# Where a weight block is split into two halves: the loads and ScalarE in place of VectorE

## The chip, the cores and the metric

One core of one Trainium2 chip runs the program. The metric is the device time of one execution in microseconds. The engines are TensorE (PE; PEld is its weight load), VectorE (DVE), ScalarE (ACT), GpSimd (POOL) and SyncE (SP), which here only issues DMAs.

## What is computed

Two layers of a hybrid backbone over 256 context tokens and 512 latent tokens of 1024 features, in float32. A norm modulated by a conditioning vector feeds one wide projection; its columns go to four token mixers (attention, Fourier mixing, a state-space scan S5, retention); each mixer's result is projected back, weighted by a gate, summed and projected once more; then comes an MLP of width 4096. Layer 1 computes the context tokens only as far as the latent ones read them.

```
for l in range(DEPTH):
    ...
    zl = split_cols(hl @ w_in[l], full_sizes)
    k_l, v_l = mla_keys(zl[0], zl[1], mla_kv_norm[l], mla_w_ukv[l], mla_qk_norm_k[l], rows, cols)
    q_l = mla_queries(zl[5], mla_q_norm[l], mla_w_uq[l], mla_qk_norm_q[l], rows, cols)
    o_a = block_softmax_attention(q_l, jnp.concatenate([k_ctx, k_l], axis=1),
                                  jnp.concatenate([v_ctx, v_l], axis=1))
    o_b = fourier_mix(zl[6])
    ...
    o_c = s5_readout(zl[2], xs_f, xs_b, cmat_f, cmat_b, s5_d[l], s5_w_glu[l])
    ...
    o_d = retention_output(o_ret, zl[8], ret_gn_w[l])
    xl_new = xl + g1 * merge_branches(o_a, o_b, o_c, o_d, zl[9], w_branch[l], w_out[l])
    xl_new = xl_new + g2 * sq_relu_mlp(ada_rms(xl_new, norm_ffn_w[l], sh2, sc2), ffn_w1[l], ffn_w2[l])

def sq_relu_mlp(h, w1, w2):
    return jnp.square(jax.nn.relu(h @ w1)) @ w2
```

## The kernel before

TensorE multiplies in a rounded form of float32 (float32r). To keep float32 accuracy, every operand is split into hi, its rounding, and lo, the remainder, and a product is three matmuls: lo by hi, hi by lo, hi by hi (`mm3`, line 299; `gemm`, line 305).

Weights lie in DRAM as blocks that the host has packed in the order of their use (`chunk_shapes`, line 86). Most are 128 partitions x 1024 float32 (512 KB): eight tiles of 128x128 of one 128-column slice of a matrix, or four of 128x256 for the second MLP matrix. Those of the branch projections are 128x256 (128 KB). A block is taken with `chunk` (line 267): `raw` (line 260) loads it on SyncE's queue into one of two buffers `raw` (one buffer `raws` for the small ones); `split` (line 290) lets ScalarE round it into `whi` and VectorE subtract into `wlo`, three buffers each (`whis` and `wlos`, two each). With `into`, tiles of a stage's own are written (`keep`, line 283: `kh`, `kl`). `fetch` (line 286) takes a block ahead of its use.

Features stand on partitions and tokens in columns, so with 128 weight columns a block gives 48 matmuls in layer 0 (24 of 512 columns, 24 of 256) and 24 of 512 columns in layer 1.

A scheduler orders the program at compile time: each engine takes what is ready by its model of time, earlier code first, and the resulting order on each engine's queue is fixed. A tile's next buffer is given when the last reader of the old one is done. Each queue then runs in order, an instruction waiting at its head for its semaphores. `issue_after` adds an edge: what the block issues on an engine comes behind a given instruction of that engine. It is used in four places that matter here. In `start` (line 557) and in `ada` (line 571), the loads on SyncE's queue stay behind the last weight load `self.last`. In `tick` (line 743), background work stays behind the last matmul, the last rounding on ScalarE and the last subtraction on VectorE. In `merge_steps` (line 846), a gate's activation stays behind the last rounding.

The order of a layer (`layer`, line 653): Fourier mixing, retention, attention, S5, and between them the gated sums (`merge_steps`, line 832: for each of 8 output tiles a gate product of one 512 KB block and a branch product of one 128 KB block; GpSimd adds the result into y, line 863). Then the output projection (8 blocks, lines 708 to 731), and the MLP (`ffn`, line 768): per group of four hidden tiles, four blocks of the first matrix, then four of the second; 64 blocks a layer. Background work is put between products by `tick`: in layer 0 the modulation of this layer and of the next (VectorE reductions over loads `adr`, `olo`, `ohi`) and the tables of S5 (`s5_prep`, partly on GpSimd). At the start (`start`, line 494) SyncE loads the first modulation's matrices `adp` and the activations `xy`, GpSimd adds up their squares, and two blocks are fetched (line 548).

GpSimd issues no DMA. It does a share of the elementwise work: adds into y, some `lo` halves of the norm (line 620), parts of S5 (lines 1562 to 1577, 1595) and its tables.

Of the kernel before, what the change touches and what calls it, by code (L numbers as in the profile page):

```python
# [9 lines left out]
F32 = mybir.dt.float32  # L10
# [4 lines left out]
OP = mybir.AluOpType  # L15
# [23 lines left out]
# ---------------------------------------------------------------- host side: layouts and shape tables  # L39
# [158 lines left out]
# ---------------------------------------------------------------- device side  # L198

class Cols:  # L200
    """a tile that holds the token columns from c0 on."""
# [8 lines left out]
class Net:  # L210
# [11 lines left out]
    # ---- small helpers  # L222
# [37 lines left out]
    def raw(self, key):  # L260
        o, n = self.off[key]
        t = self.wp.tile([128, 1024] if n > 256 else [128, 256], F32, name="raw" if n > 256 else "raws", bufs=2 if n > 256 else 1)
        src = bass.AP(tensor=self.wst.tensor, offset=self.wst.offset + o, ap=[[n, 128], [1, n]])
        self.last = self.nc.sync.dma_start(t[:, :n], src)
        return t[:, :n]

    def chunk(self, key, into=None, eng=None):
        if key in self.ahead:
            return self.ahead.pop(key)
        r = self.raw(key)  # L270
        n = r.shape[1]
        if into:
            hi, lo = (t[:, :n] for t in into)
            self.split(hi, lo, r)
            return hi, lo
        big = n > 256
        w = 1024 if big else 256
        hi = self.wp.tile([128, w], F32R, name="whi" if big else "whis", bufs=3 if big else 2)
        lo = self.wp.tile([128, w], F32R, name="wlo" if big else "wlos", bufs=3 if big else 2)
        self.last_lo = self.split(hi[:, :n], lo[:, :n], r, eng=eng)  # L280
        return hi[:, :n], lo[:, :n]
# [8 lines left out]
    def split(self, hi, lo, src, scale=None, eng=None):  # L290
        """hi + lo = src * scale, exactly, each with 12 significant bits."""
        if scale is None:
            self.last_hi = self.nc.scalar.activation(hi, src, AF.Copy)  # L293
# [5 lines left out]
    def mm3(self, out, a, b, start, stop):  # L299
        """out (+)= a^T b in float32 accuracy; a, b are (hi, lo) pairs."""  # L300
        self.mm(out, a[1], b[0], start, False)
        self.mm(out, a[0], b[1], False, False)
        self.mm(out, a[0], b[0], False, stop)

    def gemm(self, ps, w, x, segs, ks=None):
        """ps[:, 256 + t] = sum_k w[k]^T x[k][:, t]; w, x: lists over k of (hi, lo)."""
# [21 lines left out]
    def rsqrt(self, pool, src, n, scale, eps, shape=None):  # L328
        """(src * scale + eps)^-1/2 for a compact [128, n] operand."""
# [12 lines left out]
        # y (1 + e / 2 + 3 e^2 / 8), e = 1 - v y^2  # L342
# [7 lines left out]
    def horner(self, pool, w, cs, name):  # L350
        """((c0*w + c1)*w + ...)*w, last coefficient's factor included."""
# [6 lines left out]
    def expm1(self, pool, x, name):  # L358
        """(exp(x), expm1(x)) by range reduction; exp flushes to 0 below 2^-126."""
# [20 lines left out]
    def sincos(self, pool, x, name):  # L380
        """sin, cos, cos - 1 with a three-part reduction by 2 pi."""
# [23 lines left out]
    def cmul(self, pool, outr, outi, ar, ai, br, bi, conj=False, e1=None, e2=None, name="cm"):  # L405
        """(outr + i outi) = a * b, or a * conj(b)."""
# [10 lines left out]
    # ---- program  # L417
# [54 lines left out]
    # ---- adaLN  # L472
# [4 lines left out]
    def ada_fin(self, l, i, n=1, nv=2):  # L477
        """scale blocks i .. i + n - 1 are known: fold in the norm's weight."""
# [5 lines left out]
    def ada_rows(self, dst, h):  # L484
        """half h of silu(c), silu(c_ctx) on every partition: dst [128, 2, 512]."""
# [8 lines left out]
    def start(self, sp, prm):  # L494
        """the first norm; its modulation on TensorE, behind the loads."""
# [3 lines left out]
        def modulation(i, mid={}):  # L499
            """features 128 i .. 128 i + 511 for both vectors"""  # L500
# [56 lines left out]
        with self.tc.issue_after(self.last.ins):  # L557
            for _ in later:
                pass

    def ada(self, l, blocks, cs, rs, junk, acc):
        """more of the modulation on VectorE, block by block, half of the features at a time."""
# [5 lines left out]
        for n in range(len(todo) + ahead):  # L568
            if n < len(todo):
                h, i = todo[n]  # L570
                with self.tc.issue_after(self.last.ins):
# [1096 lines left out]
```

## Time and profile before

| | |
|---|---|
| time, median of 2 runs | 2301.34 us (2300.08 to 2302.6) |
| span of the profiled execution, first to last instruction | 2300.5 us |
| mean granted TensorE clock | 0.981 |
| matmuls | 12438 |
| moved by DMA | 240.26 MB |

The profile is of one execution on the chip. A busy TensorE is not TensorE at its peak: matmuls overlap and their ends are modelled, so a stretch's matmul count tells more than its busy time. Issuing a DMA does not count as busy for SyncE; GpSimd's issues, of which there are none here, would count for GpSimd.

### The profile page before, as it was taken

Reading aid. Unit: us, or ns where it says so; the run is one execution under the profiler, and the core shown is the slowest. Engines: PE = TensorE matmul, PEld = TensorE weight load, DVE = VectorE, ACT = ScalarE, POOL = GpSimd, SP = SyncE. Lnnn points to the kernel's source line nnn. Section 1 sums busy time; section 2 is a strip of 40 time slices with the busy share of each in tenths; the row PEclk is TensorE's granted clock in tenths of the full one; section 3 lists DMA queues with packets and bytes.
Section 4 is the critical chain, followed back from the end, with each engine's and each line's share of the span. In section 5 each row is a group of like instructions: output and inputs, shape, how many; then the busy total and the mean of one; then the engine's idle time right before and its main releaser. Section 6 shows DMA issues by size and latency. Waiting matters only on the chain.

```text
span 2300.5 us, 32460 instructions
## 1 busy us (share of the span) xinstructions
PE 2184.6 (95%) x12438; PEld 1856.6 (81%) x12438; DVE 1504.2 (65%) x3283; ACT 726.3 (32%) x1226; POOL 327.9 (14%) x373
## 2 busy tenths in 40 slices
PE   6988999999989999999989999999999799999999
PEld 1867988888778888888878888988777678888887
DVE  6587889976743477667795447667746756454444
ACT  2412333443223242212222235234432234322322
POOL 2061110103421010000051101100014510000000
PEclk8989999999999999999999999999999999999999
DMA  8334234312312324535322232112133232323232
GB/s 260 111 105 136 83 97 132 119 53 90 110 62 85 115 91 149 183 129 189 106 85 97 84 111 72 58 53 79 51 100 99 97 110 97 101 92 101 92 101 92
DMA packets 112027, 240.26 MB, mean 104 GB/s; under 512 B 15744, under 2 KB 43264, under 8 KB 111872
## 3 DMA queue, kind: packets, MB, share of 16 engines
q1 hardware_dynamic: 111872, 238.19, 31.9%
q8 instruction: 98, 1.61, 0.3%
q14 instruction: 57, 0.47, 0.1%
HBM read 219.21 MB, written 18.93 MB: 104 GB/s over the span
## 4 chain that ended last, share of the span: by engine, by line
PE 67%; DVE 16%; issue 5%; DMA 5%; POOL 3%; ACT 3%; SPq 0%; POOLq 0%; ACTq 0%; DVEq 0%
PE mm L239 41%; PE b L239 24%; PE b L242 3%; DMA raw<-wst 1%; DVE wlo L294 1%; DVE sx L1570 1%; DVE olo L491 1%; POOL sX L245 1%; DVE sx L1568 1%; DVE sx L245 1%; DVE S L245 1%; ACT whi L293 1%; DVE xy L255 1%; DMA par<-par 1%; DVE gate L255 1%
## 5 line engine op out<-in xcount | busy, mean ns | idle before, releaser
L239 PE MATMUL mm<-hhi,wlo 128*128 128x256 f32 (+1 forms) x1768 | 538.5, 358 | 13.1 <-DVE wlo L294 9.6
L239 PE MATMUL mm<-hlo,whi 128*128 128x256 f32 (+1 forms) x1768 | 537.5, 357 | 3.3 <-POOL hlo L245 3.2
L239 PE MATMUL mm<-hhi,whi 128*128 128x256 f32 (+1 forms) x1768 | 535.5, 356 | 0.0
L294 DVE TENSOR_TENSOR wlo<-raw,whi 128x1024 fp32r<-128x1024 f32 (+2 forms) x238 | 297.1, 1249 | 161.8 <-ACT whi L293 161.1
L239 PEld LDWEIGHTS mm<-hhi,wlo 128*128 128x128 f32 x1768 | 334.0, 190 | 61.5 <-issue 10.5
L239 PEld LDWEIGHTS mm<-hlo,whi 128*128 128x128 f32 x1768 | 334.6, 190 | 51.7 <-POOL hlo L245 6.2
L239 PEld LDWEIGHTS mm<-hhi,whi 128*128 128x128 f32 x1768 | 334.9, 190 | 46.6
L293 ACT ACTIVATE whi<-raw 128x1024 fp32r<-128x1024 f32 (+2 forms) x238 | 246.4, 1037 | 378.3 <-PE b L239 301.4
L239 PE MATMUL b<-uh,wlo 128*128 128x256 f32 (+1 forms) x704 | 216.2, 361 | 10.2 <-DVE xy L255 5.8
L255 DVE SCALAR_TENSOR_TENSOR xy<-b,mod,xy 128x256 f32<-128x256 f32 (+1 forms) x192 | 121.8, 659 | 150.2 <-PE b L239 150.1
L239 PE MATMUL b<-ul,whi 128*128 128x256 f32 (+1 forms) x704 | 215.4, 359 | 0.1
L239 PE MATMUL b<-uh,whi 128*128 128x256 f32 (+1 forms) x704 | 214.9, 358 | 0.0
L239 PEld LDWEIGHTS b<-uh,wlo 128*128 128x128 f32 x704 | 132.4, 190 | 34.6 <-ACT uh L293 6.2
L245 DVE TENSOR_TENSOR tmp<-tmp 128x768 f32<-128x768 f32 (+1 forms) x64 | 53.1, 829 | 163.6 <-ACT tmp L258 163.5
L245 POOL TENSOR_TENSOR xy<-xy,gate 128x768 f32<-128x768 f32 (+1 forms) x48 | 85.0, 1772 | 487.1 <-DVE gate L255 451.4
L239 PEld LDWEIGHTS b<-ul,whi 128*128 128x128 f32 x704 | 133.2, 190 | 21.3 <-DVE ul L294 0.6
L239 PEld LDWEIGHTS b<-uh,whi 128*128 128x128 f32 x704 | 133.2, 190 | 19.8
L258 ACT ACTIVATE tmp<-mm 128x768 f32<-128x768 f32 (+3 forms) x86 | 51.5, 599 | 289.9 <-PE mm L239 270.1
L239 PE MATMUL mm<-whi,hlo 128*128 128x256 f32 (+1 forms) x424 | 123.7, 292 | 6.0 <-DVE rpt L255 3.0
L239 PE MATMUL mm<-wlo,hhi 128*128 128x256 f32 (+1 forms) x424 | 123.7, 292 | 1.4 <-DVE wlo L294 1.4
L239 PE MATMUL mm<-whi,hhi 128*128 128x256 f32 (+1 forms) x424 | 122.4, 289 | 0.0
L258 ACT ACTIVATE gate<-mm 128x768 f32<-128x768 f32 (+1 forms) x64 | 44.8, 700 | 159.8 <-PE mm L239 159.6
(464 smaller groups left out, 3538.1 us busy)
## 6 DMA issues: line engine op xcount, KB each, us to landing
raw<-wst SPq DMA_DIRECT2D x236, 512.0 KB
adr<-wst SPq DMA_DIRECT2D x96, 256.0 KB
S<-scr SPq DMA_DIRECT2D x16, 768.0 KB
olo<-wst SPq DMA_DIRECT2D x42, 256.0 KB
adp<-wst SPq DMA_DIRECT2D x32, 256.0 KB
raws<-wst SPq DMA_DIRECT2D x64, 128.0 KB
xy<-xT SPq DMA_DIRECT2D x16, 384.0 KB
ohi<-wst SPq DMA_DIRECT2D x22, 256.0 KB
```

Of the source, the lines that this page charges most:

```text
L239: return self.nc.tensor.matmul(out, a, b, start=start, stop=stop)
L242: self.nc.tensor.transpose(out, a, self.ident[:n, :n])
L245: (eng or self.nc.vector).tensor_tensor(out=out, in0=a, in1=b, op=op)
L255: (eng or self.nc.vector).scalar_tensor_tensor(out, a, s, b, op0=op0, op1=op1)
L258: self.nc.scalar.activation(out, a, f, **kw)
L293: self.last_hi = self.nc.scalar.activation(hi, src, AF.Copy)
L294: return (eng or self.nc.vector).tensor_tensor(out=lo, in0=src, in1=hi.bitcast(F32), op=OP.subtract)
L491: self.nc.vector.tensor_tensor_reduce(out=junk, in0=r, in1=c[:, v], scale=1.0, scalar=0.0, op0=OP.mult, op1=OP.add, accum_out=acc[:, v:v + 1])
L1568: nc.vector.tensor_tensor_scan(out=Z[F, k, 1:256], data0=r8[F, 1:256], data1=W[F, k, 0:255], initial=0.0, op0=OP.mult, op1=OP.add)
L1570: nc.vector.tensor_tensor_scan(out=Z[B, k, 254::-1], data0=r8[B, 254::-1], data1=W[B, k, 255:0:-1], initial=0.0, op0=OP.mult, op1=OP.add)
```

## The change

`raw` and SyncE's weight loads are gone, and with them the buffers `raw` and `raws`. `chunk` lets GpSimd's queue load the block straight from DRAM into the float32r tile hi (the DMA casts), lets ScalarE write -hi into lo, and lets GpSimd's queue load the same block once more, added to what is in lo. `whi` and `wlo` get four buffers in place of three; the small ones keep two. Loads with `into` go the same way. All other splits, of activations, stay on ScalarE and VectorE. The orderings behind `self.last` and `self.last_lo` go; `self.last_hi` is now the negated copy of the last block, where before it was set by every split. Comments and docstrings are gone too, which is left out below.

```diff
-    def raw(self, key):
-        o, n = self.off[key]
-        t = self.wp.tile([128, 1024] if n > 256 else [128, 256], F32, name="raw" if n > 256 else "raws", bufs=2 if n > 256 else 1)
-        src = bass.AP(tensor=self.wst.tensor, offset=self.wst.offset + o, ap=[[n, 128], [1, n]])
-        self.last = self.nc.sync.dma_start(t[:, :n], src)
-        return t[:, :n]
-
     def chunk(self, key, into=None, eng=None):
         if key in self.ahead:
             return self.ahead.pop(key)
-        r = self.raw(key)
-        n = r.shape[1]
+        o, n = self.off[key]
         if into:
             hi, lo = (t[:, :n] for t in into)
-            self.split(hi, lo, r)
-            return hi, lo
-        big = n > 256
-        w = 1024 if big else 256
-        hi = self.wp.tile([128, w], F32R, name="whi" if big else "whis", bufs=3 if big else 2)
-        lo = self.wp.tile([128, w], F32R, name="wlo" if big else "wlos", bufs=3 if big else 2)
-        self.last_lo = self.split(hi[:, :n], lo[:, :n], r, eng=eng)
-        return hi[:, :n], lo[:, :n]
+        else:
+            big = n > 256
+            w = 1024 if big else 256
+            hi, lo = (self.wp.tile([128, w], F32R, name=x + ("" if big else "s"), bufs=4 if big else 2)[:, :n] for x in ("whi", "wlo"))
+        src = bass.AP(tensor=self.wst.tensor, offset=self.wst.offset + o, ap=[[n, 128], [1, n]])
+        gp = self.nc.gpsimd
+        gp.dma_start(hi, src)
+        self.last_hi = self.nc.scalar.activation(lo, hi.bitcast(F32), AF.Copy, scale=-1.0)
+        gp.dma_start(lo, src, accum_op=OP.add)
+        return hi, lo
...
         if scale is None:
-            self.last_hi = self.nc.scalar.activation(hi, src, AF.Copy)
+            self.act(hi, src)
...
-        with self.tc.issue_after(self.last.ins):
-            for _ in later:
-                pass
+        for _ in later:
+            pass
...
-                with self.tc.issue_after(self.last.ins):
-                    self.nc.sync.dma_start(rs[n % len(rs)], self.ada_src(l, i, h))
+                self.nc.sync.dma_start(rs[n % len(rs)], self.ada_src(l, i, h))
...
-            for i in (self.last_mm, self.last_hi, self.last_lo):
+            for i in (self.last_mm, self.last_hi):
```

## Rows read from the trace of the kernel before

**Rows 1.** Page, part 1: busy time, share of the span, instructions by engine.

```profile
PE 2184.6 (95%) x12438; PEld 1856.6 (81%) x12438; DVE 1504.2 (65%) x3283; ACT 726.3 (32%) x1226; POOL 327.9 (14%) x373
```

**Rows 2.** Layer 1 MLP: length, PE, PEld, DVE, ACT, POOL busy, clock, DMA, GB/s.

```profile
1968.40:2296.90 328.50, 328.49 (x1440) 269.06 (x1439) 155.93 (x179) 90.64 (x116) 0.00 (x0) 1.00 0.30 97
```

**Rows 3.** Pieces of the chain in order of time: start us, us, what.

```profile
890.61 33.92 PE mm L239 x192
...
1696.30 34.33 PE mm L239 x162
...
1850.20 37.79 PE mm L239 x166
...
1903.41 3.47 DMA raw<-wst
...
1990.39 21.76 PE mm L239 x96
```

**Rows 4.** Six of forty equal slices; columns as in rows 2.

```profile
0.00:57.50 57.50, 40.23 (x108) 10.01 (x109) 34.52 (x172) 16.39 (x24) 12.83 (x11) 0.88 0.80 260
...
115.00:172.50 57.50, 46.91 (x261) 39.95 (x259) 49.21 (x138) 7.78 (x14) 37.26 (x49) 0.88 0.35 104
...
345.00:402.50 57.50, 53.40 (x318) 46.45 (x319) 54.81 (x188) 21.90 (x48) 4.46 (x2) 1.00 0.41 131
...
862.50:920.00 57.50, 57.50 (x327) 49.88 (x326) 41.60 (x88) 12.07 (x13) 0.00 (x0) 1.00 0.46 150
...
1150.00:1207.50 57.50, 50.98 (x287) 43.63 (x286) 53.44 (x138) 12.46 (x17) 32.38 (x47) 0.94 0.28 84
...
1782.50:1840.00 57.50, 43.43 (x215) 35.53 (x215) 44.24 (x70) 15.64 (x32) 33.16 (x38) 0.91 0.29 97
```

**Rows 5.** The chain that ended last, shares of the span by line.

```profile
by line: PE mm L239 41.2%; PE b L239 23.6%; issue 5.1%; PE b L242 2.6%; DMA raw<-wst 1.5%; DVE wlo L294 1.5%; DVE sx L1570 1.0%; DVE olo L491 1.0%; POOL sX L245 0.9%; DVE sx L1568 0.8%; DVE sx L245 0.7%; DVE S L245 0.6%; ACT whi L293 0.6%; 
```

**Rows 6.** SyncE's issues on line 264: duration in ns, first and last start.

```profile
L264 SPq DMA_DIRECT2D raw<-wst x256: 327/328/927, 35.9 to 2272.3; - x128
L264 SPq DMA_DIRECT2D raws<-wst x64: 322/328/1417, 57.8 to 1882.3; - x64
```

**Rows 7.** Groups by line and shape: busy us, mean ns, idle before and releasers.

```profile
L294 DVE TENSOR_TENSOR wlo<-raw,whi 128x1024 fp32r<-128x1024 f32 x224 | 285.7, 1275 | 144.0 <-ACT whi L293 143.3 <-DMA M<-strip 0.3
L293 ACT ACTIVATE whi<-raw 128x1024 fp32r<-128x1024 f32 x224 | 236.1, 1055 | 372.9 <-PE b L239 301.4 <-DMA raw<-wst 27.6 <-PE mm L239 24.1
...
L294 DVE TENSOR_TENSOR wlos<-raws,whis 128x256 fp32r<-128x256 f32 x64 | 36.3, 566 | 11.5 <-ACT whis L293 11.2
...
L245 POOL TENSOR_TENSOR xy<-xy,gate 128x512 f32<-128x512 f32 x24 | 38.1, 1588 | 239.1 <-DVE gate L255 239.1
```

**Rows 8.** Instructions on the tile wlo in those slices: PE, PEld, DVE.

```profile
115.00:172.50 57.50, 17.77 (x62) 13.04 (x62) 3.65 (x3) 0.88 0.35 104
...
1897.50:1955.00 57.50, 19.31 (x58) 10.72 (x58) 4.89 (x4) 1.00 0.30 100
...
sum 2300.00, PE 914.42 PEld 569.64 DVE 297.15; mean PE 22.86 PEld 14.24 DVE 7.43
```

**Rows 9.** Instructions on the tile wlos in those slices: PE, PEld, DVE.

```profile
115.00:172.50 57.50, 3.14 (x12) 2.18 (x12) 1.74 (x4) 0.88 0.35 104
...
1897.50:1955.00 57.50, 0.00 (x0) 0.00 (x0) 0.00 (x0) 1.00 0.30 100
...
sum 2300.00, PE 61.12 PEld 37.16 DVE 36.25; mean PE 1.53 PEld 0.93 DVE 0.91
```

**Rows 10.** A split of the layer 1 MLP in the timeline.

```profile
2013.83 1.23 DVE L294 TENSOR_TENSOR wlo<-raw,whi 128x1024 fp32r<-128x1024 f32 x1 [0.25 <-ACT whi L293]
```

**Rows 11.** The page's fourth part: the chain's shares by engine.

```profile
PE 67%; DVE 16%; issue 5%; DMA 5%; POOL 3%; ACT 3%; SPq 0%; POOLq 0%; ACTq 0%; DVEq 0%
```

**Rows 12.** The longest wait in the layer 1 MLP: us in total, times, longest.

```profile
ACT whi L293 <- PE b L239: 120.6, 29, 4.4
```

**Rows 13.** TensorE's waits over the span: us in total, times, longest.

```profile
PE mm L239 <- DVE wlo L294: 11.0, 6, 4.3
```

## The prediction

> **What bounds the kernel now.** I read the engine shares first, then the time slices, then the chain, and only then the groups by shape. The reader is to see in [rows 1] that TensorE counts as busy for 95% of the span, VectorE for 65% and GpSimd for 14%: what is taken off VectorE pays only where TensorE stands or runs below its pace. The stretch in [rows 2] is the MLP of layer 1: TensorE is busy 328.49 of 328.50 us, VectorE 156, GpSimd 0. It is at its bound, and its 1440 matmuls make 60 weight blocks (24 matmuls each), so a block is wanted every 328.5 / 60 = 5.47 us; the chain says the same (96 matmuls, 4 blocks, in 21.76 us [rows 3]). In layer 0, with 256 more columns, 192 matmuls take 33.92 us, 8.5 us a block [rows 3]. Elsewhere it is different: at 115, 345, 1150 and 1782 us TensorE is busy 43 to 53 of 57.5 us, with VectorE at 44 to 55 [rows 4]. The chain gives the splits' subtraction 1.5% of the span (34.5 us), and the landing of raw blocks as much [rows 5]. So about 35 us hang on the work that is removed, and 116 us (2300.5 less 2184.6 [rows 1]) is all that TensorE idles; 2% of the time is 46 us.
>
> **What the change does to a block.** Now SyncE issues the load in 0.33 us [rows 6], it lands 3.47 us after the issue began [rows 3], ScalarE rounds it in 1.055 us and VectorE subtracts in 1.275 us [rows 7], each on a queue of its own. After it, GpSimd issues a casting load into hi, ScalarE writes -hi into lo, and GpSimd issues an adding load into lo. The ScalarE instruction has the shape of the one it replaces, so it costs nothing new. VectorE loses 224 subtractions of 128x1024 (285.7 us), 64 of 128x256 (36.3 us) [rows 7] and a few of other shapes.
>
> **The gain.** I take the chain's 34.5 us [rows 5]. Its ends are 0, because where weights are late the subtraction (1.275 us) gives way to a second landing, and 133 us: the split time in the 19 slices, the first and last of the forty left out, where TensorE is busy under 56 of 57.5 us (107 us on large blocks, 25 on small ones, more on rounding; the first and last of the 19 and the sum over all forty stand in [rows 8, 9]).
>
> **The loss.** GpSimd's queue takes its turns in order. The adding load waits at its head for ScalarE's copy, which waits for the casting load's landing; behind it stand the next block's casting load and GpSimd's own adds. If block n's two loads stand next to each other, GpSimd has one turn per block, and no number of buffers shortens it. Four buffers (three before) give a lead of three blocks, once per stretch.
>
> The turn, T, is put together from four parts, since the trace has no load issued by GpSimd and none that casts or adds. First the casting load's landing: 3.47 us, less SyncE's 0.33, plus GpSimd's issue. The ends for that issue are SyncE's 0.33 us [rows 6] and 1.59 us, the mean of GpSimd's 128x512 add [rows 7]; I take 1.0, about midway. That makes 4.14 us. Second, the casting load queues behind the adding load issued just before it. A plain block holds the 16 DMA engines for 0.30 x 5.47 = 1.64 us [rows 2]. The ends are 0 (gone during the issue) and 3.28 less 1.0 us, if an adding load holds them twice as long; I take 0.35, about half of what the issue leaves of a plain load. Third, ScalarE: 1.055 us [rows 7] and a hand-over of 0.25 us, as the subtraction shows behind its copy [rows 10]. Fourth, the issue of the adding load, 1.0 us.
>
> T = 4.14 + 0.35 + 1.31 + 1.0 = 6.8 us. By the low ends it is 3.14 + 0.33 + 1.31 + 0.33 = 5.1 us, under the pace of 5.47, and nothing is lost. By the high ones it is 3.14 + 1.59 + 1.69 + 1.31 + 1.59 = 9.3 us (an issue of 1.59 leaves 1.69 of the 3.28).
>
> Layer 1, MLP: 60 x (6.8 - 5.47) = 80 us. Ends: 0 and 60 x 3.83 = 230.
>
> Layer 0, MLP: 8.5 us a block covers 6.8, so nothing. If the modulation's loads, with which the DMA share is 0.46 already [rows 4], stretch T above 8.5, that cover is gone at the price of the excess per block.
>
> Layer 1, gates beside branch products: a pair is 24 + 6 matmuls of 0.227 us (21.76 / 96), 6.8 us. GpSimd issues four loads (4.0 us), waits once for landing and copy (3.14 + 1.31; the small block's wait lies inside it) and adds into y (1.59 us), 10.0 us, 3.2 too many. The two undisturbed stretches of the chain, 34.33 and 37.79 us [rows 3], hold 10.6 pairs: 34 us, less some 9 for the buffers' lead, 25. Ends: 0 and 10.6 x (12.4 - 6.8) = 59. In layer 0 a pair is wider (8.5 + 2 us) and covers the 10.0.
>
> Start: DMA is 0.80 busy at 260 GB/s in the first slice [rows 4], and TensorE stands for 17 us of it. Four buffers of 512 KB are now filled twice, 2.1 MB more: 8 us. Ends: 0 and 16.
>
> GpSimd's own work: 640 issues of 1.0 us (2 x 320 loads [rows 6]) make it busy a further 28% of the span, in front of work that holds 3% of the chain, 69 us [rows 11], some 60 steps of about a microsecond. I take 0.25 us a step, 15 us. Ends: 0 and 60.
>
> Costed at nothing: SyncE's queue without weights (the modulation's loads may go earlier and hold up no weights there) and the dropped ordering behind the subtraction, which is gone. TensorE's full stretches hide both; uncovered, each moves background work alone.
>
> Sum: -34.5 + 80 + 0 + 25 + 8 + 15 = +93.5 us on the profiled span of 2300.5 us: 2394, called **2395 us**. The median of the runs, 2301.34, is 0.8 us above that span, which I leave out.
>
> **A rule weighed.** What a plain block costs the DMA engines is the share of 0.30 in [rows 2]; an adding load this trace does not have. The Trainium skill, "Collectives: The Full Stack", Part 3 on why ReduceScatter is half of AllGather, says that an add inside a transfer is slow not for its arithmetic but because it must read two sources, so its read traffic is twice a copy's. By that the turn would be near 8.7 us and the time near rival C's. No run here shows it yet.
>
> **Rivals.** A, hidden: the compile-time order puts the next casting load ahead of the waiting adding load, so landing and copy overlap across blocks, and 5.47 us need hold two issues and the transfers alone. For it: ScalarE's split already waits 120.6 us in that stretch for a buffer that TensorE has to free [rows 12], so blocks are early now. Against it: a casting load is ready only when TensorE frees a block, every 5.47 us, and the copy is ready some 5.45 us (4.14 + 1.31) after its own casting load, a close race. The time: 2300.5 - 34.5 + 8 + 8 (half of GpSimd's 15) = 2282 us.
>
> B, faster: as A, and VectorE sets the pace of the mixers, so half of the 133 us of splits in the low slices comes off. For it: VectorE at 49 to 55 of 57.5 us at 115, 345 and 1150 us [rows 4]. Against it: part of that is background work that nobody waits for, and TensorE waits for large splits directly only 11.0 us in all [rows 13]. 2300.5 - 66 = 2235 us; it passes 2% from about a third of the 133 us on.
>
> C, DMA engines: the adding load holds them twice as long as a plain one. A block then takes 3 x 0.30 = 0.90 of them at the present pace, the casting load waits 2.28 us in place of 0.35, T is 8.7 and the layer 1 MLP loses 60 x 3.26 = 196; the gates lose 1.93 more a pair (45 in all), the start 16. 2300.5 - 34.5 + 196 + 45 + 16 + 15 = 2538 us. For it: two reads. Against it: the share of 0.30 also counts waits inside transfers, which might overlap.
>
> D: a load into float32r may keep all bits of the weight, hi then being the weight itself and lo zero. Instructions and bytes stay the same, so it changes no time and has no chance of its own.
>
> **How the numbers follow.** Forecast 0.46 (its own range 2350 to 2470), A 0.29, B 0.13, C 0.12. About 2% is what a measurement of this kernel can tell from no change. Faster by over 2% is B, 0.13; within 2% is A, 0.29; slower is the forecast and C, 0.58. The range reaches down past A to 2262 and leaves B out; upwards all high ends together, with no gain, give 2300.5 + 230 + 59 + 16 + 60 = 2666, and I stop at 2640: about 0.8 held.
>
> **What would show it.** Right: in the layer 1 MLP TensorE idles before matmuls on wlo, some 1.3 us a block, released by a DMA into wlo; GpSimd's adding loads are released by ScalarE, and its casting loads begin just behind them and not at TensorE's release; the layer 0 MLP keeps its length; VectorE is near 1504 - 322 = 1182 us. Wrong: that stretch still at 328.5 us (A); mixers shorter by more than 35 us (B); a DMA share of 0.9 in the layer 1 MLP (C); GpSimd's issues far off 1.0 us, which shifts every term. A lower granted clock where TensorE starts to wait, as at 1782 us (0.91 [rows 4]), would hide inside T.

## The result, and the profile after

The changed kernel takes 2584.36 us (median of 2 runs, 2577.64 to 2591.08) against 2301.34: a ratio of 1.1228, 95% interval 1.1203 to 1.1253, so 283 us more. The profiled execution spans 2575.9 us at a mean granted clock of 0.939 (before 2300.5 and 0.981). The forecast was 2395 us, in a range of 2262 to 2640: the sign is right, the time lies inside the range, but the size is a third of what came.

Of the changed kernel's page, the engine shares (part 1), the DMA queues (part 3: packets, MB, share of 16 engines' span) and the issues (part 6: KB each, median us from issue to landing):

```profile
PE 2265.4 (88%) x12438; PEld 1900.7 (74%) x12438; DVE 1190.1 (46%) x2963; ACT 730.7 (28%) x1226; POOL 753.9 (29%) x1013
...
q0 software_dynamic: 92160, 276.90, 48.9%
q1 hardware_dynamic: 65792, 99.74, 12.2%
...
whi<-wst POOLq DMA_DIRECT2D x224, 512.0 KB, 6.0
wlo<-wst POOLq DMA_DIRECT2D x224, 512.0 KB, 5.5
...
whis<-wst POOLq DMA_DIRECT2D x64, 128.0 KB, 3.7
wlos<-wst POOLq DMA_DIRECT2D x64, 128.0 KB, 5.3
```

Against [rows 1], VectorE lost what it was to lose (1504 to 1190 us, forecast 1182), and GpSimd is busy 426 us longer with its 640 issues. TensorE's share fell from 95 to 88%: it waits, and what it does is slower, since the clock fell. A large casting load lands 6.0 us after its issue (median), where one plain load on the chain took 3.47 [rows 3].

GpSimd's issues by form (busy us, mean ns | idle us before them and its releasers), which answer to SyncE's in [rows 6]:

```profile
L275 POOL DMA_DIRECT2D wlo<-wst x238 | 207.8, 873 | 966.1 <-ACT wlo L274 786.4 <-ACT wlos L274 80.3 <-ACT tmp L258 22.2
L273 POOL DMA_DIRECT2D whi<-wst x238 | 167.1, 711 | 460.3 <-PE mm L239 318.6 <-PE b L239 126.4 <-PE b L242 10.2
```

The adding loads of the large blocks (line 275) make GpSimd's queue stand for 966 us, 867 of them for ScalarE's negated copies (786 for large blocks, 80 for small ones).

To see where the time went, the timeline is cut at marks that both kernels have: the first matmul on a weight block, the reload of x ahead of each output projection, the first and last rounding of a hidden tile (`uh`) in each layer, the last store of layer 0. Lengths in us; "two casts" and the others to the right are runs of the next section.

| stretch | before | after | two casts (e2) | copy, no add (e3) | add, free copy (e7) | order back (e6) | two casts, order back (e8) |
|---|---|---|---|---|---|---|---|
| start | 54.4 | 68.4 | 64.2 | 64.0 | 68.9 | 69.2 | 63.0 |
| layer 0, mixers and gates | 686.8 | 733.3 | 699.6 | 715.9 | 731.4 | 729.7 | 695.8 |
| layer 0, output projection | 100.3 | 106.5 | 100.9 | 102.6 | 101.8 | 105.9 | 100.9 |
| layer 0, MLP | 519.5 | 591.3 | 552.3 | 561.4 | 569.6 | 556.3 | 520.4 |
| layer 0's last products | 21.3 | 23.9 | 21.1 | 22.7 | 20.9 | 22.6 | 21.1 |
| layer 1, mixers and gates | 509.5 | 561.7 | 502.1 | 523.2 | 527.8 | 557.9 | 499.8 |
| layer 1, output projection | 67.6 | 85.2 | 67.4 | 73.1 | 67.2 | 84.7 | 67.4 |
| layer 1, MLP | 316.9 | 379.4 | 317.9 | 332.4 | 316.3 | 378.1 | 318.0 |
| end | 24.2 | 26.2 | 24.6 | 24.6 | 24.2 | 26.7 | 24.7 |

So of 275 us the layer 1 MLP has 62 (forecast 80), the layer 0 MLP 72 (forecast 0), the mixers with their gates 46 and 52, the output projections 24 and the start 14.

**The turn.** In the layer 1 MLP of the changed kernel (window row: length, PE, PEld, DVE, ACT, POOL busy, clock, DMA share, GB/s):

```profile
2170.19:2549.64 379.45, 334.73 (x1406) 269.05 (x1405) 84.86 (x118) 96.09 (x122) 83.45 (x118) 0.95 0.72 162
```

Its waits (us in total, times, longest):

```profile
POOL wlo L275 <- ACT wlo L274: 245.8, 57, 8.3
ACT wlo L274 <- DMA whi<-wst: 244.2, 48, 8.2
...
POOL whi L273 <- PE b L239: 40.9, 12, 6.3
...
PE b L239 <- ACT uh L258: 30.5, 9, 6.8
...
PE mm L239 <- ACT tmp L258: 7.5, 5, 1.9
```

And one turn in its timeline (start us, us, what [idle before <-releaser]), first GpSimd, then ScalarE:

```profile
2206.36 0.88 POOL L275 DMA_DIRECT2D wlo<-wst  x1 [1.88 <-ACT wlo L274]
2206.91 0.89 POOL L273 DMA_DIRECT2D whi<-wst  x1
2214.55 0.85 POOL L275 DMA_DIRECT2D wlo<-wst  x1 [6.76 <-ACT wlo L274]
2215.09 0.87 POOL L273 DMA_DIRECT2D whi<-wst  x1
```

```profile
2213.20 1.06 ACT L274 ACTIVATE wlo<-whi 128x1024 fp32r<-128x1024 f32 x1 [7.14 <-DMA whi<-wst]
2214.16 0.58 ACT L258 ACTIVATE tmp<-mm 128x512 f32<-128x512 f32 x1
```

This is the in-order turn of the forecast: adding load, casting load 0.55 us behind it, 6.29 us until ScalarE can copy, 1.06 for the copy, 0.29 to the next adding load; together 8.19. The median of the 21 such intervals in the stretch is 8.27. Yet with 118 issues, 59 blocks, in this window a block takes only 379.45 / 59 = 6.43 us, because the compiled order is not strictly in pairs. It repeats, every three blocks, casting, adding, casting, casting, adding, adding: two blocks share a turn, and the second adding load follows the first after 2.82 us (median of 19). Two turns and 2.8 us make three blocks, 19.4 us or 6.45 a block.

TensorE doesn't wait for wlo, as the forecast had it, but for `uh` and `tmp`: the Relu at 2214.16 stood behind a copy that waited 7.14 us for a landing, though the last matmul of its product had ended by 2211.2. The waits in the rows are 38 of the 62 us; TensorE's busy time itself grows by 17.8 us, with the granted clock at 0.95: around those stops it is at 1.2 GHz in place of 2.4.

**The layer 0 MLP.** Waits in its first 300 us:

```profile
POOL wlo L275 <- ACT wlo L274: 183.0, 24, 16.3
...
ACT uh L258 <- DVE tmp L245: 92.9, 15, 15.2
DVE adu L486 <- DMA adr<-wst: 54.1, 27, 5.6
...
PE b L239 <- ACT uh L258: 42.1, 8, 7.4
```

And how the longest come about (timeline, VectorE, then ScalarE, then GpSimd):

```profile
981.61 0.69 DVE L486 CUSTOM_DVE_ANT_0 adu<-adr,adc 128x512 bf16<-128x512 f32 x1 [1.45 <-DMA adr<-wst]
...
987.19 0.69 DVE L486 CUSTOM_DVE_ANT_0 adu<-adr,adc 128x512 bf16<-128x512 f32 x1 [4.88 <-DMA adr<-wst]
...
987.81 0.95 DVE L245 TENSOR_TENSOR tmp<-tmp 128x768 f32<-128x768 f32 x1
```

```profile
977.04 0.80 ACT L258 ACTIVATE tmp<-mm 128x768 f32<-128x768 f32 x1
988.80 0.84 ACT L258 ACTIVATE uh<-tmp 128x768 fp32r<-128x768 f32 x1 [10.96 <-DVE tmp L245]
989.54 1.04 ACT L274 ACTIVATE wlo<-whi 128x1024 fp32r<-128x1024 f32 x1
```

```profile
991.77 0.86 POOL L275 DMA_DIRECT2D wlo<-wst  x1 [12.93 <-ACT tmp L258]
```

A square on VectorE, ready at 977.84, stands behind the modulation's reductions, which stand for their load. ScalarE's rounding of the hidden tile waits for the square, the negated copy stands behind that, and the adding load behind the copy and, by its row, the Relu after it. Each queue is held by the head of another. In the kernel before, `tick` kept these reductions behind the last subtraction of a weight block; in the compiled order the longest run of them in this MLP was 6, in the changed one 10.

**The gates of layer 1.** One pair of gate and branch block (timeline, GpSimd):

```profile
2062.19 0.90 POOL L275 DMA_DIRECT2D wlo<-wst  x1 [4.75 <-ACT wlos L274]
2062.79 1.20 POOL L275 DMA_DIRECT2D wlos<-wst  x1
2063.34 1.22 POOL L273 DMA_DIRECT2D whi<-wst  x1
2063.88 1.22 POOL L273 DMA_DIRECT2D whis<-wst  x1
2064.44 1.98 POOL L245 TENSOR_TENSOR xy<-xy,gate 128x512 f32<-128x512 f32 x1
2071.09 0.89 POOL L275 DMA_DIRECT2D wlo<-wst  x1 [4.67 <-ACT wlos L274]
```

Four loads, one addition and one wait: 8.9 us a pair, where 6.8 are needed. Behind layer 0's S5 a pair takes 10.4 us in both kernels.

### The profile page after: what moved, and what is told of

It is laid out like the page before. It is cut to its first block, busy times and chain, and to the rows that moved or that the text cites. A ratio compares the mean times of both kernels' runs of the same rounds, so it can differ in the third digit from the quotient of the medians.

```text
span 2575.9 us, 32924 instructions
## 1 busy us (share of the span) xinstructions
PE 2265.4 (88%) x12438; PEld 1900.7 (74%) x12438; DVE 1190.1 (46%) x2963; ACT 730.7 (28%) x1226; POOL 753.9 (29%) x1013
## 5 line engine op out<-in xcount | busy, mean ns | idle before, releaser
L239 PE MATMUL mm<-hhi,wlo 128*128 128x256 f32 (+1 forms) x1768 | 545.5, 362 | 53.9 <-ACT gate L258 27.4
L274 ACT ACTIVATE wlo<-whi 128x1024 fp32r<-128x1024 f32 (+2 forms) x238 | 247.2, 1039 | 932.4 <-DMA whi<-wst 856.9
L275 POOL DMA_DIRECT2D wlo<-wst x238 | 207.8, 873 | 966.1 <-ACT wlo L274 786.4
L273 POOL DMA_DIRECT2D whi<-wst x238 | 167.1, 711 | 460.3 <-PE mm L239 318.6
L239 PE MATMUL b<-uh,wlo 128*128 128x256 f32 (+1 forms) x704 | 225.4, 376 | 85.4 <-ACT uh L258 77.1
L239 PE MATMUL b<-ul,whi 128*128 128x256 f32 (+1 forms) x704 | 223.8, 372 | 2.0 <-DVE ul L289 2.0
L239 PE MATMUL b<-uh,whi 128*128 128x256 f32 (+1 forms) x704 | 222.4, 370 | 0.0
L239 PEld LDWEIGHTS b<-uh,whi 128*128 128x128 f32 x704 | 139.5, 198 | 21.5
L486 DVE CUSTOM_DVE_ANT_0 adu<-adr,adc 128x512 bf16<-128x512 f32 x128 | 88.2, 689 | 56.6 <-DMA adr<-wst 54.1
L255 DVE SCALAR_TENSOR_TENSOR gate<-gate,mm 128x768 f32<-128x768 f32 (+1 forms) x48 | 39.3, 818 | 150.9 <-PE mm L239 127.1
```

The lines of the kernel that those rows point to most:

```text
L239: return self.nc.tensor.matmul(out, a, b, start=start, stop=stop)
L255: (eng or self.nc.vector).scalar_tensor_tensor(out, a, s, b, op0=op0, op1=op1)
L273: gp.dma_start(hi, src)
L274: self.last_hi = self.nc.scalar.activation(lo, hi.bitcast(F32), AF.Copy, scale=-1.0)
L275: gp.dma_start(lo, src, accum_op=OP.add)
L486: self.nc.vector.tensor_tensor_reduce(out=junk, in0=r, in1=c[:, v], scale=1.0, scalar=0.0, op0=OP.mult, op1=OP.add, accum_out=acc[:, v:v + 1])
```

## The experiments

All are timed beside the kernel before; ratios are to it, with their 95% intervals. The diffs are against the changed kernel unless they say otherwise.

**e1, e2, e3, e4: which part costs?**

```diff
# e1
-        self.last_hi = self.nc.scalar.activation(lo, hi.bitcast(F32), AF.Copy, scale=-1.0)
+        self.last_hi = self.nc.vector.tensor_scalar(lo, hi.bitcast(F32), -1.0, None, op0=OP.mult)
# e2
-        gp.dma_start(hi, src)
-        self.last_hi = self.nc.scalar.activation(lo, hi.bitcast(F32), AF.Copy, scale=-1.0)
-        gp.dma_start(lo, src, accum_op=OP.add)
+        self.last_hi = gp.dma_start(hi, src)
+        gp.dma_start(lo, src)
# e3
-        gp.dma_start(lo, src, accum_op=OP.add)
+        gp.dma_start(lo, src)
# e4, against the kernel before
-        self.last = self.nc.sync.dma_start(t[:, :n], src)
+        self.last = self.nc.gpsimd.dma_start(t[:, :n], src)
```

> The negated copy goes to VectorE, all else as in the changed kernel (2584). If ScalarE's order is what costs (its copies wait for a landing and the Relus and splits of finished products stand behind them), the waits of TensorE for uh in the L1 MLP (30.5 us in 9) go and the whole comes to 2480 to 2540. If GpSimd's own turn sets the pace (adding load waits for the copy, next casting load behind it), the turn is as long with the copy on either engine: 2560 to 2610. A third case: VectorE's squares and residual sums now stand behind the waiting copy instead, and it is slower than 2610.

Measured: 2593.34 us, ratio 1.1271 (1.1234 to 1.1308), the layer 1 MLP 411.0 us. With the copy on VectorE TensorE's weight loads still wait 36.4 us for `uh` in that stretch (changed kernel 34.7). For the whole it matters little which engine's queue is held, so the turn is the better theory; but the layer 1 MLP is 32 us longer than with the copy on ScalarE, so it is not the turn alone. (`last_hi` is now on VectorE: background work there stands behind the copy, and the orderings on ScalarE are off.)

> Both loads of a block are plain casting loads and the negated copy is left out, so the low half is wrong (it is the high half again) and no load waits for any engine but for a free buffer. If the waits cost (GpSimd's turn, ScalarE's order), the whole comes back to 2270 to 2330 and the L1 MLP to 315 to 330 us. If it is the loads themselves (twice the weight traffic, software issue on GpSimd), most of the 283 us stay: 2450 to 2570.

Measured: 2354.95 us, 1.0235 (1.0191 to 1.0278). Most of the loss goes with the waits and the adding, and the layer 1 MLP is back at 317.9. It misses its mark by 25 us: 33 of what is left lie in the layer 0 MLP, which neither answer named. (`last_hi` is the casting load here and in e8 and e14, so its orderings hold on GpSimd and not on ScalarE.)

> The negated copy stays and the second load is a plain casting load that overwrites it (low half wrong): all waits stand, only the addition goes. If the waits are the cause, as good as no change: 2540 to 2590. If the adding load's own traffic is the cause (it reads two sources), its landing falls below the 5.5 us of the changed kernel and the whole to 2400 or less.

Measured: 2426.49 us, 1.0546 (1.0490 to 1.0601): between the two answers. The waits alone make 70 us over e2 (spans 2419.9 and 2350.0); the addition makes 156 more.

> The kernel before, with its plain weight loads issued on GpSimd's queue instead of SyncE's, the split on ScalarE and VectorE as before. If issuing on GpSimd by itself costs (its own arithmetic in retention, MLA and S5 stands behind loads that wait for a buffer, and loads behind it), 2340 to 2420, with the growth in the mixers and S5 and none in the MLPs. If the queue is innocent and only the change's waits between two loads cost: 2295 to 2320.

Measured: 2328.84 us, 1.0121 (1.0092 to 1.0151). That lies between the two answers. Issuing from GpSimd by itself costs 26 us, 15 of them in the mixers and 5 at the start, none in the layer 1 MLP. (With `last` on GpSimd the modulation's loads on SyncE are no longer kept behind the weight loads, so a part may be that.)

**e5, e6, e8: the lost ordering; e7: the adding without the wait.**

```diff
# e5, against the kernel before; likewise in start and in ada
-            for i in (self.last_mm, self.last_hi, self.last_lo):
+            for i in (self.last_mm, self.last_hi):
# e6; last_dve is VectorE's last residual sum or split. e8 is e2 with the same
-            for i in (self.last_mm, self.last_hi):
+            for i in (self.last_mm, self.last_hi, self.last_dve):
# e7
-        self.last_hi = self.nc.scalar.activation(lo, hi.bitcast(F32), AF.Copy, scale=-1.0)
+        self.last_hi = self.nc.scalar.activation(lo, self.ident[:, 0:1].to_broadcast([128, n]), AF.Copy, scale=0.0)
```

> The kernel before with only the orderings dropped that the change drops: the modulation's loads behind weight loads, the background work behind VectorE's last weight subtraction. The subtractions themselves stay on VectorE, and so does their own place in its queue. If the lost ordering is what made the layer 0 MLP longer (33 us with two plain casting loads and no wait at all), that stretch (519.5 us) grows by 15 to 40 here too and the whole is 2315 to 2345. If the growth comes from the second load's traffic, nothing changes: 2295 to 2308.

Measured: 2326.07 us, 1.0101 (1.0072 to 1.0130), the layer 0 MLP 533.9, 14 more than before, just short of the 15 expected: the lost orderings (of the modulation's loads and of the background work) cost in the old kernel too, if less.

> The changed kernel with the background work ordered behind VectorE's last residual sum or split again, as a stand-in for the ordering that went with the subtraction. If the modulation's runs of up to 10 instructions ahead of a square hold up TensorE, the layer 0 MLP falls from 591 us to 550 to 565 and the whole to 2540 to 2560. If GpSimd's turn alone sets that stretch, it stays at 585 to 595.

Measured: 2537.34 us, 1.1018 (1.0968 to 1.1068), the layer 0 MLP 556.3: of the 45 us by which the span gets shorter (2575.9 to 2531.2) 35 come back there.

> Two plain casting loads, no copy (low half wrong), with the ordering of the background work behind VectorE again: no split on any engine and no wait, the best that could come of taking the splits off VectorE. If the lost ordering is the cause of the layer 0 MLP's 33 us, that stretch is at 520 to 530 us and the whole at 2318 to 2330. If splits on VectorE had cost the 34 us of the chain, the rest would now show it: below 2290.

Measured: 2318.18 us, 1.0082 (1.0060 to 1.0103), the layer 0 MLP 520.4. The lost ordering is nearly the whole of e2's 33 us. And with no weight split on any engine and no load waiting for another, the kernel is still 16 us slower than before. Against that kernel the relief of VectorE and ScalarE shows only in layer 1's mixers, 499.8 against 509.5. Against e4, which issues from GpSimd too and keeps the splits, those mixers lose 16.7 us and the span 15.6 (2326.7 to 2311.1): a gain is there, with the second load's price inside it, and the 26 us that e4 costs outweigh it.

> ScalarE fills lo from a constant, with an instruction as long as the negated copy that waits for no landing; the adding load stays (low half wrong: the weight itself is added to zero). So the two loads of a block no longer wait for each other, only their traffic and the adding stay. If the turn (landing, copy, issue in a row) is the cause of what the adding load costs, 2350 to 2400, near the two plain casting loads (2355). If the adding load's hold on the DMA engines is the cause, 2480 to 2570, with the layer 1 MLP at 350 us or more.

Measured: 2433.74 us, 1.0568 (1.0524 to 1.0613): between the answers again, since the stretches answer differently. In the layer 1 MLP the adding alone costs nothing. Its window rows in e2, e3 and e7, in this order:

```profile
2007.57:2325.50 317.93, 317.25 (x1405) 260.42 (x1405) 84.90 (x118) 38.10 (x63) 62.21 (x118) 1.00 0.62 195
```

```profile
2062.91:2395.32 332.41, 321.98 (x1406) 263.60 (x1405) 84.90 (x118) 97.86 (x121) 62.37 (x118) 0.98 0.60 185
```

```profile
2087.64:2403.96 316.32, 316.32 (x1404) 260.30 (x1403) 84.89 (x118) 96.94 (x121) 82.89 (x118) 1.00 0.94 196
```

Over 317.9 us the wait alone adds 14.5, the adding alone nothing, both together 61.5. That is how a turn behaves: without the adding it lasts 6.7 us (median of 21) and costs little in an order where two of three blocks share one; the adding load, which the next casting load queues behind, lengthens it to 8.3. The same rows give an estimate of the adding load's price. At a DMA share of 0.62 two casting loads hold the engines for 0.62 x 317.93 / 59 = 3.3 us a block, 1.7 each, as much as the 1.64 of a plain load. At 0.94 the block holds them 5.0, so the adding load 3.4: twice a plain one. (In the changed kernel's own row, 0.72 x 379.45 / 59 = 4.6, it is 3.0.) In layer 0's mixers, where the modulation's loads share the engines, the adding costs without a wait for a landing too: 731.4 in e7 against 699.6 in e2.

**e9, e10: the next casting load ahead of the waiting adding load.** With e6's ordering; `then` gives the next block's key, in e9 in the MLPs alone, in e10 everywhere but in the blocks with `into`.

```diff
-        gp.dma_start(hi, src)
-        self.last_hi = self.nc.scalar.activation(lo, hi.bitcast(F32), AF.Copy, scale=-1.0)
-        gp.dma_start(lo, src, accum_op=OP.add)
+        hi = self.high(key)[0]
+        k = self.then(key)
+        after = self.high(k)[1]
+        self.early[k] = (self.early_hi, after)
+        self.last_hi = self.nc.scalar.activation(lo, hi.bitcast(F32), AF.Copy, scale=-1.0)
+        with self.tc.issue_after(after.ins):
+            gp.dma_start(lo, self.wsrc(key), accum_op=OP.add)
```

> The changed kernel with VectorE's ordering back and, in the two MLPs alone, each adding load queued on GpSimd behind the next block's casting load, so that the next landing and copy run while this block's adding load waits. Same traffic, result complete. If the in-order turn (8.2 us with a casting load's landing inside it) is the cause in the MLPs, two blocks share a turn: the layer 1 MLP falls from 379 us to 316 to 330, the layer 0 MLP from 556 to 525 to 545, and the whole to 2430 to 2480. If traffic sets them, the layer 1 MLP stays over 360.

Measured: 2472.55 us, 1.0733 (1.0705 to 1.0761). The layer 1 MLP's row:

```profile
2119.10:2450.10 331.00, 319.92 (x1406) 262.45 (x1405) 84.87 (x118) 97.39 (x121) 84.04 (x119) 0.99 0.90 188
```

Same loads, same bytes, another order on one queue: 47 of e6's 61 us are gone, just past the expected 330. The layer 0 MLP is at 547.1, just short of its mark. What is left there is likely the hold on the DMA engines: two casting loads leave 1 us (e8), this order 28.

> The same one block ahead for all weight blocks, the mixers too. If the turn is the cause there as well, the layer 1 mixers (557.9 us) fall to 515 to 530 and the layer 0 part up to the reload of x (729.7) to 700 to 715: 2370 to 2420 in all. If the adding load's hold on the DMA engines and GpSimd's own work behind its issues are what is left there, the mixers stay within 15 us of the run with the MLPs alone.

Measured: 2479.41 us, 1.0763 (1.0717 to 1.0809). Layer 1's mixers stay at 559.1 (e9 563.2), layer 0's get longer, 748.9 after 728.5, by more than the 15 us that the second answer allows. So this order gains nothing in the mixers as a whole. In layer 1's gates it does: from the last scan matmul to the reload of x 60.1 us after 67.4 in e9 (before 54.7), and between the same five gate activations ahead of S5 27.8 after 36.0 (before 25.5). Of the 15 us that it gains there 11 are lost again in the rest of the layer's mixers, and no run shows by what.

**e11 to e15: GpSimd's own arithmetic.** In S5 each step of the scan passes through GpSimd twice. From layer 0's S5 stage of the changed kernel (timeline, GpSimd):

```profile
629.98 0.60 POOL L273 DMA_DIRECT2D whi<-wst  x1
630.57 0.56 POOL L273 DMA_DIRECT2D whis<-wst  x1
631.12 1.88 POOL L245 TENSOR_TENSOR xy<-xy,gate 128x768 f32<-128x768 f32 x1
632.94 0.75 POOL L245 TENSOR_TENSOR Z<-Z,Y 96x256 f32<-96x256 f32 x1
637.90 0.90 POOL L275 DMA_DIRECT2D wlos<-wst  x1 [4.21 <-ACT wlos L274]
638.85 0.88 POOL L275 DMA_DIRECT2D wlo<-wst  x1
640.06 0.74 POOL L245 TENSOR_TENSOR sx<-sx 128x256 f32<-128x256 f32 x1 [0.33 <-DVE sx L245]
```

The scan's next rotation (`sx`) comes behind two adding loads and the 4.21 us that the first waits, but it is not held by them: its row has it wait 0.33 us for VectorE. The hold is on ScalarE, in the same window:

```profile
637.18 0.42 ACT L274 ACTIVATE wlos<-whis 128x256 fp32r<-128x256 f32 x1 [5.92 <-DMA whis<-wst]
637.50 1.04 ACT L274 ACTIVATE wlo<-whi 128x1024 fp32r<-128x1024 f32 x1
638.45 0.40 ACT L258 ACTIVATE Z<-Z 96x256 f32<-96x256 f32 x1
```

GpSimd's product `Z` was done at 633.69; the tanh on it stands behind two copies that wait for a landing, and VectorE's next steps (`sd`, then `sx`) stand behind the tanh. VectorE's wait for it over layer 0's S5 stage (us in total, times, longest), in the kernel before, the changed one, e9 and e12:

```profile
DVE sd L255 <- ACT Z L258: 5.6, 6, 1.1
DVE sd L255 <- ACT Z L258: 30.4, 5, 8.8
DVE sd L256 <- ACT Z L259: 30.2, 5, 7.6
DVE sd L256 <- ACT Z L259: 2.1, 4, 0.6
```

GpSimd's own S5 steps that begin right behind a load which waited have only some 9 us of such waits in front of them in both layers.

```diff
# e11, against the kernel before
-        self.last_lo = self.split(hi[:, :n], lo[:, :n], r, eng=eng)
+        i = self.split(hi[:, :n], lo[:, :n], r, eng=eng if big else self.nc.gpsimd)
+        if big:
+            self.last_lo = i
# e12 (on e9), e13 (on the kernel before), e14 (on e8); likewise for X, Z and the memsets
-            self.tt(W[:, 0], t1[:, 0], t1[:, 1], OP.subtract, gp)
-            self.tt(W[:, 1], t2[:, 0], t2[:, 1], OP.add, gp)
+            self.tt(W[:, 0], t1[:, 0], t1[:, 1], OP.subtract)
+            self.tt(W[:, 1], t2[:, 0], t2[:, 1], OP.add)
# e15 (on e12), and tick and gates no longer behind last_hi
+        if key[0] in ('f1', 'f2', 'wo') or into:
             self.last_hi = self.nc.scalar.activation(lo, hi.bitcast(F32), AF.Copy, scale=-1.0)
+        else:
+            gp.tensor_scalar(lo, hi.bitcast(F32), -1.0, None, op0=OP.mult)
```

> The kernel before with only the subtractions of the 64 small blocks (128x256, 36 us of VectorE) on GpSimd, which has no loads to issue there. If VectorE bounds the mixers, 2285 to 2297. If GpSimd's own adds behind them cost as much as VectorE gains, 2298 to 2312.

Measured: 2324.32 us, 1.0095 (1.0077 to 1.0113), worse than either answer, with 20.7 us more in layer 0's mixers. From layer 0's S5 to the reload of x GpSimd's subtractions wait 70.1 us for ScalarE's rounding, with GpSimd's other steps behind them, and over the span they take GpSimd 59.3 us where VectorE took 36.3. Work put in front of GpSimd's own steps is paid for, even without a single load on the queue; how much is the waits and how much the work, this run doesn't separate.

> The changed kernel with one block ahead in the MLPs, VectorE's ordering back, and now the S5 scan's arithmetic (rotations, the product ahead of the tanh) on VectorE instead of GpSimd. If that arithmetic stands on GpSimd behind the loads' issues and the adding loads' waits, the S5 stages, 20 to 35 us too long in each layer, get 12 to 30 us of it back each: 2415 to 2450 against 2473. If not, or if VectorE becomes the bound of the scan, 2460 to 2500.

Measured: 2445.33 us, 1.0631 (1.0595 to 1.0667), some 27 us better than e9; from the first load of `ex` to the last scan matmul layer 0's S5 stage falls from 146.4 to 129.8 us and layer 1's, short of the 12 us expected, from 178.3 to 171.0. With the product `Z` on VectorE the wait of `sd` for the tanh is down from 30.2 to 2.1 us (rows above), so a good part of the gain is likely on ScalarE's queue and not on GpSimd's; no run shows it apart.

> The kernel before with the same arithmetic of the S5 scan on VectorE, as the other half of the comparison: here GpSimd's queue holds no loads, and VectorE also has the weight splits. If VectorE is as busy as its 44 to 55 of 57.5 us in slices say, slower: 2305 to 2330. If the hand-overs between the two engines cost more than VectorE's time, faster: 2280 to 2298.

Measured: 2289.09 us, 0.9945 (0.9924 to 0.9965). The best of all: faster than both kernels, if by half a per cent. So the move that gains 27 us in e12 gains 10 here, without any load on GpSimd's queue. Layer 0's S5 stage has most of it (118.5 to 110.0 us).

> Two plain casting loads, no copy (low half wrong), VectorE's ordering back, and the S5 scan's arithmetic on VectorE: no wait but for buffers is left on GpSimd. The layer 0 S5 stage with its attention is 20 us longer than before without this move although no load waits for another. If the issues in front of GpSimd's arithmetic cost that, 2290 to 2305 against 2318. If it is the second load's traffic, 2312 to 2325.

Measured: 2314.70 us, 1.0052 (1.0034 to 1.0069). Layer 0's S5 stage gains 4.9 us (139.6 to 134.7), the whole hardly anything: without waits the issues in front of the arithmetic are not the main cost, and the expected 2290 to 2305 was wrong. The time lies in the range named for the second load's traffic, which no run takes apart.

> As the run with one block ahead in the MLPs and the S5 scan's arithmetic on VectorE, and now, in the mixers alone, the negated copy on GpSimd itself, so that no other engine's queue holds an instruction that waits for a landing. If ScalarE's queue is what is left in the mixers (its copies wait 90 us for landings in the S5 and gates stage of layer 1, with the gates' tanh and the scan's steps behind them), the layer 1 mixers fall from 550.8 to 520 to 538 us. If GpSimd's turn is the bound there, it is longer with the copy inside it, and they come to 555 or more.

Measured: 2536.47 us, 1.1012 (1.0980 to 1.1044), layer 1's mixers 599.1 after 550.8. The copy of a 128x1024 block takes GpSimd 2.89 us (ScalarE 1.06): a longer turn costs the mixers too, and freeing ScalarE's queue doesn't make up for it. The dropped orderings are in this time as well.

## Why the prediction was wrong in its size

Between the forecast span, 2394 us, and the measured one lie 182 us. The layer 0 MLP has 72 of them, the mixers 59 beyond the 40 forecast for gates and GpSimd's own work, the gain that did not come 34, the output projections 24, the start and the ends of the layers 11; the layer 1 MLP takes 18 off.

**Where the bound lies, and the turn: right.** GpSimd's in-order turn through landing, copy and issue is what bounds the layer 1 MLP and the gates. The order alone shows it, e9 in the MLP and e10 in the gates.

**The turn's length: mis-sized by the adding load.** T was put at 6.8 us and is 8.3. Without the adding it is 6.7, so the sum was right for a second load that only loads, in part because issues shorter than forecast offset a longer landing; the step that failed is the second part, "I take 0.35", the wait of a casting load behind the adding load. With issues of 0.55 us in place of 1.0 and 6.29 us from issue to copy in place of 4.49, the landing took 1.8 us more. That is rival C's mechanism, given 0.12: an adding load holds the engines about twice as long, 3.4 us against 1.7 (e7, e2). By the rule that the prediction weighed (the Trainium skill, "Collectives: The Full Stack", Part 3: an add inside a transfer has to read two sources) it would be twice, and the trace agrees.

**Layer 1 MLP: 80 forecast, 62 measured, from two errors that offset.** The turn is longer, and the order is half of rival A's, with two of three blocks in one turn. Strictly in pairs, 60 blocks at 8.27 us would have cost 60 x (8.27 - 5.47) = 168.

**Layer 0 MLP: 0 forecast, 72 measured; the largest miss.** Two steps failed. "Costed at nothing: ... the dropped ordering behind the subtraction, which is gone": it kept the modulation's reductions from standing in front of the squares, and its loss is 35 us (e6) or 32 (e2 against e8). And "8.5 us a block covers 6.8": the text named the case that it would not and gave it no price. In e6, with the ordering back, 37 us of the loss are left. The median interval between adding loads in its first 300 us, beside the modulation's loads, is 8.6 us (11.2 in the changed kernel, where the reductions are in it), so the cover is just gone there; but by the matmuls done (1624, before 1697) that part costs only some 13 us. What costs the rest behind it, no run shows.

**Gates of layer 1: right in the sum, 25 forecast and 24 measured.** A pair takes 8.9 us, forecast 10.0, and the buffers' lead of 9 us didn't come. The stretch behind S5, from the last scan matmul to the reload of x, grew by 14.0 us (54.7 to 68.7), the five gate activations ahead of it by 10.4 (25.5 to 35.9). The output projection, which the sum left out, grew by 17.6: its blocks have the same turn, and without the wait (e7) it is at 67.2.

**The start: 8 forecast, 14 measured.** 4.6 of it come with the issue from GpSimd alone (e4), 4 to 5 more with the second load (e2, e3, e8), the rest with the adding.

**GpSimd's own work: 15 forecast, the mixers' other 74 us measured.** The issues are cheaper than taken (0.71 and 0.87 us, 0.55 from one to the next). The term priced issues and no waits, and that is the step that failed: moving the scan's steps away gets some 27 us back with waits (e12), 10 in the kernel before, hardly any with loads that do not wait (e14). That GpSimd's steps themselves stand behind waiting loads is the smaller part by the rows, some 9 us; the scan also stands on ScalarE behind copies that wait, which the sum did not have at all.

**The gain: 34.5 forecast, none in the whole.** e8, without any split or wait, is 10 us ahead of the kernel before in layer 1's mixers and 16 behind in all; against e4, on the same queue, it is 15.6 ahead with the second load's price inside it. The step that failed is taking the chain's share of the subtraction as gain in full and with nothing against it for issuing from GpSimd.

**What stays open.** In e12 the mixers are still 22 and 41 us longer than before. e7 and e3 show that the landing's wait and the adding both have part in it; how much of the rest is ScalarE's queue, held by waiting copies, how much GpSimd's, and how much the DMA engines, no run separates. A queue for the adding load other than GpSimd's was not tried: the Trainium skill, "DMA: Bandwidth & Descriptors", on SWDGE vs HWDGE vs iDMA, says that only GpSimd issues loads that cast or add, and no run here shows otherwise.

## What to carry to other kernels

If a load waits for the result of an earlier load on the same in-order queue, as here, that makes the landing part of that queue's turn: price the whole turn, then read the compiled order to see how many blocks share one, and put the next block's first load ahead of the wait. Before an instruction is removed, look for what was ordered behind it; here that ordering was worth as much as the subtraction's share of the chain. And count what else lives on the queues, of the engine that issues and of the one that copies: in this kernel moving the scan's steps off GpSimd pays by itself, 2289 us against 2299 beside it.

## What the runs showed of the hardware

An adding load of 512 KB held the DMA engines some 3.4 us (3.0 by the changed kernel's row), a casting one 1.7 (e7, e2) and a plain one 1.64 [rows 2]. GpSimd's issue has a duration of 0.55 to 0.89 us in the layer 1 MLP of the changed kernel, but where two follow each other the next one starts 0.55 us behind. A landing that took 3.47 us from SyncE (one load) took 3.8 from GpSimd for the same plain load (e4, median of 236), 4.0 to 4.9 for two casting loads (e2) and 6.0 where an adding load runs ahead of it.
